# RWKV scan: gram and state products over 64 of the 128 rows, four head pairs to a step, and the scan's first load tied behind a v tile

## The chip, the cores and the metric

The kernel runs on one core of a Trainium2 chip. The metric is the device time of one execution in microseconds (us), lower is better. Three timed runs of the kernel before gave 3011.88, 3013.64 and 3014.78 us, median 3013.64.

## The reference

The model is a two-layer decoder trunk: layer 0 mixes tokens with an RG-LRU block, layer 1 with RWKV-7 time mixing; each layer then has cross-attention into 256 memory tokens and a squared-ReLU MLP (1024 tokens, width 1024, everything float32). The change is inside the RWKV-7 mixer of layer 1, in this recurrence with 16 heads of size 64:

```python
def step(state, inp):
    r_t, w_t, k_t, v_t, a_t, b_t = inp
    sa = jnp.einsum('bhij,bhj->bhi', state, a_t)
    state = (state * w_t[:, :, None, :] + sa[..., None] * b_t[:, :, None, :]
             + v_t[..., None] * k_t[:, :, None, :])
    y_t = jnp.einsum('bhij,bhj->bhi', state, r_t)
    return state, y_t
```

## The kernel before

The mixer first computes k, r and v as 128-feature tiles (`fphase`, one tile of 128 features, that is two heads, per turn), with a lot of preparation between; results go to DRAM tensors (`STd`: the two row operands of a head, b-like and k-like; `MVd`: the a-like and r-like operands; `XTd`: the inverted triangular matrices; `Vd`, `G1d`, `G2d`). In the v turns `evac_v` transposes the finished v tile, stores it to `Vd` (line 1402) and stores the gate terms to `G1d` and `G2d` (line 1416). All these transfers are issued on SyncE's queue (SP), in order.

Then the **scan** runs over 16 chunks of 64 tokens. Features of a head pair q (0 to 7) lie on the 128 partitions, head h = 0 on rows 0 to 63 and h = 1 on rows 64 to 127 (`hr[h]`). `load(n)` fetches the operands of chunks 2n and 2n+1: `st` (lines 1446, 256-byte pieces), `mv` (line 1450) and the triangular matrices (line 1452); `load_late(n)` fetches v (line 1468) and the gates (line 1472). In one chunk:

- **gram** (`scan_gram`, one chunk ahead): for each pair q and head h a product of the pair's `st` columns with `mv` of that head (line 1497). `mv` is padded: a tile `[8, 2, 2, 128]` whose other head's rows are set to zero once (line 1438), so that a product over all 128 rows gives the sums of one head. VectorE multiplies the result by masks into a tile `gt` (lines 1500 and 1503), ScalarE copies `mv` rows into it (line 1502), and the scaled `st` is transposed (line 1511) and copied in by ScalarE (line 1512).
- **W** (line 1589), one product per head over 128 rows: `gt` times `sv`, where `sv` holds the state on the head's own rows and v on the other 64. Its copy (line 1591) feeds **U** (line 1609, 64 rows by 64 columns).
- The **state product of y** (line 1594): `mv` times `sv`, over all 128 rows with the zero padding.
- VectorE writes U times a diagonal into `sv` (line 1611); **S** (line 1617) gives the new state, which VectorE adds into the next chunk's `sv` (line 1619); the output product (line 1625) adds into y.

All float32 products are two instructions each in the trace. The order of instructions on each engine is set by a scheduler that simulates the program and takes what is ready by program order; `self.behind()` pins what is issued in its block behind the last instruction of the same engine in program order. `load(0)` is called after the v turn of tile 6 (`LD = 6`); the scheduler may issue it earlier, as soon as buffers are free. Data tiles are 45 buffers `u` of 4 KB per partition, and two larger buffers `z` (of `half_big`) that hold `mv`, and before that the g2 operands of the v turns (`lowr`).

Of the kernel before, what the change touches and what calls it, by code (L numbers as in the profile page):

```python
# [10 lines left out]
ALU = mybir.AluOpType  # L11
# [1091 lines left out]
def rwkv(self, X, xt, lw_wa, lw_g, post):  # L1103
    nc, I = self.nc, self.I
    mm = nc.tensor.matmul
# [5 lines left out]
    MVd, STd = (self.dram([128, 8, 2, 1024]) for _ in range(2))  # L1111
# [13 lines left out]
    for hf in range(2):  # L1125
        o = hf * 512
# [12 lines left out]
        if hf:  # L1139
            h = maps[0][2]  # L1140
# [4 lines left out]
    h = maps[1][2]  # L1145
# [10 lines left out]
    hr = [slice(0, 64), slice(64, 128)]  # L1156
# [166 lines left out]
    def aside(step):  # L1323

        for fn, steps in ((solve_load, SL), (solve, SO), (solve_store, ST), (merge, ME), (merge_load, ML), (merge_store, MS)):
            for i, at in enumerate(steps):
                if at == step:
                    with (self.behind() if fn != solve else ExitStack()):
                        fn(i)
# [18 lines left out]
    def early(f):  # L1348
        ld[f] = self.unit()
        nc.sync.dma_start(ld[f], Pd[f * 128:f * 128 + 128, :])  # L1350
# [77 lines left out]
    cst, prs, z, mvb = {}, {}, [], []  # L1428

    def load(n):  # L1430

        if n >= 8:
            return
        ts = slice(n * 128, n * 128 + 128)
        if n < 2:
            mv = self.half_big([8, 2, 2, 128])
            for h in range(2):
                nc.gpsimd.memset(mv[hr[1 - h], :, h, :, :], 0.0)
            mvb.append(mv)
        mv = mvb[n % 2]  # L1440
        sts = []
        for g in range(2):
            st = self.unit().rearrange("p (e q w t) -> p e q w t", e=2, q=4, w=2)
            for e in range(2):
                es = slice(n * 128 + e * 64, n * 128 + e * 64 + 64)
                nc.sync.dma_start(st[:, e], STd[:, 4 * g:4 * g + 4, :, es])
            sts.append(st)
        for h in range(2):
            for w in range(2):
                nc.sync.dma_start(mv[hr[h], :, h, w, :], MVd[hr[h], :, w, ts])  # L1450
        xu = self.unit().rearrange("p (q t) -> p q t", t=128)
        nc.sync.dma_start(xu, XTd[:, :, ts])
        pcs = self.unit().rearrange("p (e q t) -> p e q t", e=2, q=8)
        for e in range(2):
            c, cs = 2 * n + e, slice(e * 64, e * 64 + 64)
            cst[c] = dict(st=[t[:, e] for t in sts], mv=mv[:, :, :, :, cs], xt=xu[:, :, cs],
                          pcs=pcs[:, e], pcc=self.pc[:, c * 8:c * 8 + 8].unsqueeze(2), gts=[])

    def load_late(n):

# [23 lines left out]
            qs = slice(4 * g, 4 * g + 4)  # L1484
            nc.gpsimd.tensor_tensor(scv[:, qs], s["st"][g], s["pcc"][:, qs].unsqueeze(3).broadcast_to([128, 4, 2, 64]), ALU.mult)

    def scan_gram(c, groups):
        if c >= 16:
            return
        s = cst[c]  # L1490
        for g in groups:
            gt = self.unit()[:, 0:768].rearrange("p (q h w) -> p q h w", q=2, h=2)
            pv = self.bank().rearrange("p (q h w) -> p q h w", q=2, h=2)
            for pp in range(2):
                q = 2 * g + pp
                for h in range(2):
                    mm(pv[:, pp, h, :], s["st"][q // 4][:, q % 4].rearrange("p w t -> p (w t)"), s["mv"][:, q, h], start=True, stop=True)
            for h in range(2):
                o = hr[1 - h]
                nc.vector.tensor_tensor(gt[o, :, h, 0:64], pv[o, :, h, 0:64],  # L1500
                                        self.mask2[o].unsqueeze(1).broadcast_to([64, 2, 64]), ALU.mult)
                nc.scalar.copy(gt[hr[h], :, h, 0:64], s["mv"][hr[h], 2 * g:2 * g + 2, h, 0, :])
            nc.vector.tensor_tensor(gt[:, :, :, 64:128], pv[:, :, :, 64:128],
                                    self.mask1[:, 0:64].unsqueeze(1).unsqueeze(1).broadcast_to([128, 2, 2, 64]), ALU.mult)
            if c < 15:
                if g % 2 == 0:
                    s["tp"] = self.bank().rearrange("p (q h i) -> p q h i", q=4, h=2)
                tp = s["tp"][:, 2 * (g % 2):2 * (g % 2) + 2]
                for pp in range(2):
                    q = 2 * g + pp  # L1510
                    nc.tensor.transpose(tp[:, pp].rearrange("p h i -> p (h i)"), s["sc"][:, q * 128:q * 128 + 128], self.ident)
                nc.scalar.copy(gt[:, :, :, 128:192], tp)
            s["gts"].append(gt)


    yq = lambda t: t.rearrange("p (q i) -> p q i", i=64)
# [18 lines left out]
    def post_norm(c):  # L1535
        s = cst[c]
        y = s["y"]
        mean, var = s["n"]
        POST(nc).tensor_tensor(yq(y[:, 0:512]), yq(y[:, 0:512]), over(var), ALU.mult)
# [17 lines left out]
    for i, fs in enumerate(turns):  # L1557
        for f in turns[i + 1] if i < 6 else []:
            early(f)
        self.fphase(I["b_w_rkv"][0, 2], fs, xv, evac_v, spread=i == 0)  # L1560
        aside(len(TURNS) + 6 + i)
        if fs[-1] == LD:
            load(0)
    scan_scale(0)
    scan_gram(0, range(4))
    load_late(0)
    self.depth, self.ahead = 2, 3
    self.psum_layout(0, 8)
# [2 lines left out]
    for c in range(16):  # L1571
        if c % 2 == 0:
            with (ExitStack() if c else self.behind()):
                load(c // 2 + 1)
                load_late(c // 2 + 1)
        s = cst[c]
        sv, gts, mv, pcc, xtc, pcs = s["sv"], s["gts"], s["mv"], s["pcc"], s["xt"], s["pcs"]
        dbv = self.db[:, 0:128].rearrange("p (q a t) -> p q a t", a=2, t=8)[:, :, c % 2, c // 2:c // 2 + 1]
        gt_of = lambda q: gts[q // 2][:, q % 2]
        W, U, S, wsb = [], [], [], []  # L1580
        y = self.unit()
        yp = self.bank()
        Y = yp.rearrange("p (q i) -> p q i", i=64)
        for m in range(2):
            ph = self.bank()
            reg = [ph[:, x * 256:x * 256 + 256].rearrange("p (q i) -> p q i", i=64) for x in range(2)]
            W.append(reg[0]); U.append(reg[1]); S.append(reg[0])
            for q, h in heads:
                mm(W[m][hr[h], q, :], gt_of(m * 4 + q)[:, h, 0:64], sv[:, m * 4 + q, h, :], start=True, stop=True)
            w_ = y[:, 512 + m * 256:768 + m * 256].rearrange("p (q i) -> p q i", i=64)  # L1590
            nc.scalar.copy(w_, W[m])
            wsb.append(w_)
            for q, h in heads:
                mm(Y[hr[h], m * 4 + q, :], mv[:, m * 4 + q, h, 1, :], sv[:, m * 4 + q, h, :],
                   start=(m == 0 and q == 0), stop=False)
            if c < 15:
                for h in range(2):
                    nc.gpsimd.tensor_tensor(pcs[hr[h], m * 4:m * 4 + 4, :], sv[hr[h], m * 4:m * 4 + 4, h, :],
                                            pcc[hr[h], m * 4:m * 4 + 4].broadcast_to([64, 4, 64]), ALU.mult)
        scan_scale(c + 1)  # L1600
        scan_gram(c + 1, (0, 1))
        if c > 1:
            flip_out(c - 2)
        if c:
            post_var(c - 1)
        for m in range(2):
            qs = slice(m * 4, m * 4 + 4)
            for q, h in heads:
                mm(U[m][hr[h], q, :], xtc[hr[h], m * 4 + q, :], wsb[m][hr[h], q, :], start=True, stop=True)
            for h in range(2):  # L1610
                nc.vector.tensor_tensor(sv[hr[h], qs, h, :], U[m][hr[h]], dbv[hr[h], qs].broadcast_to([64, 4, 64]), ALU.mult)
        scan_gram(c + 1, (2,))
        if c < 15:
            for m in range(2):
                qs = slice(m * 4, m * 4 + 4)
                for q, h in heads:
                    mm(S[m][hr[h], q, :], gt_of(m * 4 + q)[:, h, 128:192], sv[:, m * 4 + q, h, :], start=True, stop=True)
                for h in range(2):
                    nc.vector.tensor_add(cst[c + 1]["sv"][hr[h], qs, h, :], pcs[hr[h], qs, :], S[m][hr[h]])
        scan_gram(c + 1, (3,))  # L1620
        if c:
            post_norm(c - 1)
        for m in range(2):
            for q, h in heads:
                mm(Y[hr[h], m * 4 + q, :], gt_of(m * 4 + q)[:, h, 64:128], sv[:, m * 4 + q, h, :], start=False,
                   stop=(m == 1 and q == 3))
        nc.scalar.copy(y[:, 0:512], yp)
        s["y"] = y
        post_mean(c)
# [5 lines left out]
    w = I["b_w_o"][0]  # L1635
# [54 lines left out]
```

## Time and profile before

| what | value |
|---|---|
| median of three runs | 3013.64 us |
| the profiled execution | 3011.39 us, span 3009.7 us, mean granted clock 0.98 |
| busy share of the span | PE 95%, PEld 79%, DVE 60%, ACT 45%, POOL 38% |
| the scan | first W at 1817.05 us, end near 2013 us |
| distance from chunk to chunk in the middle of the scan | 12.1 and 12.3 us in turn |

PE is the matrix unit, PEld its weight loads, DVE VectorE, ACT ScalarE, POOL GpSimd, SPq SyncE's queue of transfers. A row of the timeline gives the start (us from the span's start), the length, the engine, the line and a count of merged instructions; in brackets the idle time of the engine before it and who ended it. A row of the table by stretches gives the busy time of each engine, PEclk (the granted clock of the matrix unit as a share of full speed), the busy share of the 16 DMA engines, and what they moved in GB/s.

### The profile page before, as it was taken

To read this page: it belongs to the slowest core of one execution; us is meant where nothing else is said; L and a number is where in the kernel's file an instruction comes from. 1 tells how busy PE (TensorE), PEld (TensorE's weight loads), DVE (VectorE), ACT (ScalarE), POOL (GpSimd) and SP (SyncE) were. 2 spreads that over 40 slices of the span, in tenths; PEclk is the share of its full clock that TensorE was granted. 3 is DMA by queue.
4 is the path that set the end of the run, shared out by engine and by line. 5 is a ranking of instruction groups with operands and counts; after the bars stand their busy time and mean duration, and the time that the engine had idled before them with its cause. 6 is when DMAs were issued, how large, how long until landed. Compare 5 with 4: busy or idle time off the path is not lost. (4 is left out here: it accounts for less than half of the span.)

```text
span 3009.7 us, 42878 instructions
## 1 busy us (share of the span) xinstructions
PE 2867.0 (95%) x16987; PEld 2382.3 (79%) x16987; DVE 1811.5 (60%) x1996; ACT 1357.9 (45%) x1943; POOL 1152.8 (38%) x1055
## 2 busy tenths in 40 slices
PE   7999999898999999989999899989999899999998
PEld 6888798786888878877877578878888688887886
DVE  5576552547345688867785536884354744568776
ACT  6464342535455543347442534442243545454332
POOL 2000100015666664431486225651001556667442
PEclk9999999998999999999999999999999999999999
DMA  8213261122444564332656889852312244455443
GB/s 258 73 46 94 88 210 60 57 84 70 153 154 152 213 225 146 119 116 89 183 155 183 220 246 228 175 127 96 100 50 77 84 140 154 154 210 203 158 136 119
DMA packets 382889, 421.93 MB, mean 140 GB/s; under 512 B 91248, under 2 KB 293216, under 8 KB 382688
## 3 DMA queue, kind: packets, MB, share of 16 engines
q1 hardware_dynamic: 370656, 379.19, 42.0%
q0 software_dynamic: 11568, 39.41, 3.5%
q8 instruction: 134, 2.20, 0.3%
q14 instruction: 67, 0.55, 0.1%
q10 hardware_dynamic: 464, 0.59, 0.1%
HBM read 284.31 MB, written 134.74 MB: 139 GB/s over the span
## 5 line engine op out<-in xcount | busy, mean ns | idle before, releaser
L204 DVE TENSOR_TENSOR u<-u,u 128x1024 fp32r<-128x1024 f32 (+1 forms) x518 | 818.6, 1608 | 355.3 <-ACT u L203 335.3
L304 PE MATMUL p<-u,u 128*128 128x512 f32 (+1 forms) x1920 | 716.7, 376 | 18.2 <-ACT u L203 9.5
L203 ACT CAST u<-u 128x1024 fp32r<-128x1024 f32 (+1 forms) x550 | 542.7, 1024 | 421.4 <-PE q L305 158.7
L305 PE MATMUL p<-u,u 128*128 128x512 f32 (+1 forms) x1920 | 718.1, 374 | 9.4 <-DVE u L204 9.4
L306 PE MATMUL p<-u,u 128*128 128x512 f32 (+1 forms) x1920 | 714.9, 373 | 3.8 <-DVE u L204 3.7
L304 PE MATMUL q<-u,u 128*128 128x512 f32 (+1 forms) x1632 | 642.5, 395 | 25.2 <-ACT u L203 8.3
L305 PE MATMUL q<-u,u 128*128 128x512 f32 (+1 forms) x1632 | 638.5, 392 | 7.0 <-DVE u L204 7.0
L306 PE MATMUL q<-u,u 128*128 128x512 f32 (+1 forms) x1632 | 633.6, 391 | 0.0
L304 PEld LDWEIGHTS p<-u,u 128*128 128x128 f32 x1920 | 366.5, 191 | 84.5 <-ACT u L203 13.5
L305 PEld LDWEIGHTS p<-u,u 128*128 128x128 f32 x1920 | 367.6, 191 | 74.5 <-DVE u L204 14.6
L306 PEld LDWEIGHTS p<-u,u 128*128 128x128 f32 x1920 | 367.2, 191 | 67.4 <-DVE u L204 5.8
L315 POOL TENSOR_SCALAR s<-s 128x1 f32<-128x1 f32 x98 | 36.1, 369 | 992.2 <-ACT u L313 991.2
L304 PEld LDWEIGHTS q<-u,u 128*128 128x128 f32 (+1 forms) x1632 | 308.3, 190 | 97.0 <-ACT u L203 13.5
L305 PEld LDWEIGHTS q<-u,u 128*128 128x128 f32 (+1 forms) x1632 | 308.8, 189 | 73.0 <-DVE u L204 9.3
L306 PEld LDWEIGHTS q<-u,u 128*128 128x128 f32 (+1 forms) x1632 | 308.3, 189 | 64.4
L431 POOL TENSOR_TENSOR u<-u,u 128x1024 f32<-128x1024 f32 x64 | 179.2, 2823 | 86.5 <-DVE u L204 80.4
L976 DVE TENSOR_TENSOR z<-z,q 128x512 f32<-128x512 f32 x192 | 128.9, 681 | 90.4 <-PE q L306 90.2
L204 POOL TENSOR_TENSOR u<-u,u 128x1024 fp32r<-128x1024 f32 x32 | 95.0, 2968 | 164.0 <-ACT u L203 101.9
L411 POOL TENSOR_TENSOR u<-u,u 128x512 f32<-128x512 f32 x96 | 150.8, 1580 | 2.9
L927 POOL TENSOR_TENSOR u<-u,u 128x512 f32<-128x512 f32 x32 | 47.1, 1471 | 166.2 <-ACT u L916 160.1
L304 PE MATMUL q<-z,u 128*128 128x512 f32 x256 | 102.1, 399 | 7.0 <-DVE u L611 7.0
L611 DVE SCALAR_TENSOR_TENSOR u<-p,s,u 128x1024 f32<-128x1024 f32 x24 | 30.8, 1284 | 122.1 <-ACT u L203 77.9
(260 smaller groups left out, 3536.5 us busy)
## 6 DMA issues: line engine op xcount, KB each, us to landing
u<-d SPq DMA_DIRECT2D x198, 512.0 KB, 4.4
d<-u SPq DMA_DIRECT2D x109, 512.0 KB, 3.5
d<-u POOLq DMA_DIRECT2D x68, 512.0 KB, 4.1
d<-u SPq DMA_DIRECT2D x132, 256.0 KB, 3.7
u<-in_m_w_up SPq DMA_DIRECT2D x64, 512.0 KB, 5.8
u<-in_m_w_down SPq DMA_DIRECT2D x64, 512.0 KB, 5.9
u<-in_c_w_kv SPq DMA_DIRECT2D x32, 512.0 KB, 6.5
u<-d SPq DMA_DIRECT2D x56, 256.0 KB, 6.1
```

The costliest lines, as they stand in the source:

```text
L203: self.nc.scalar.copy(hv, src)
L204: (eng or self.nc.vector).tensor_tensor(lv, src, hv, ALU.subtract)
L304: mm(o, ah, bh, start=first, stop=False, **kw)
L305: mm(o, ah, bl, start=False, stop=False, **kw)
L306: mm(o, al, bh, start=False, stop=last, **kw)
L315: nc.gpsimd.tensor_scalar(v, ss, 1.0 / n, eps, ALU.mult, ALU.add)
L411: sub = lambda o, x, y: nc.gpsimd.tensor_tensor(o, x, y, ALU.subtract)
L431: self.nc.gpsimd.tensor_tensor(f[o][i], f[x][i], f[y][i], ALU.subtract)
L611: nc.vector.scalar_tensor_tensor(o, src, r, gb, ALU.mult, ALU.mult)
L927: tt(s1, r21, r22, ALU.add)
L976: nc.vector.tensor_add(to_, to_, o)
```

## The change

The `mv` tile is unpadded: head h keeps its own 64 rows, a chunk pair's `mv` is half as large, two lie in one `z` buffer, and the zero fills on POOL go. The gram products and the state products of y read only the 64 rows of their head, so they are 64x128 and 64x64 instead of 128x128 and 128x64 (rows by weight columns). The results of h = 0 and h = 1 of the gram go to separate PSUM banks. `scan_gram` handles four pairs at once instead of two: one call does 8 products, four mask multiplies of 256 elements per row (two of them were 128), two copies of `mv`, four transposes and one copy of 512. The fourth `gt` tile goes (three tiles per chunk, sorted by purpose). `load(0)` is put behind the last instructions of the v turn of tile 6, and `mv` is fetched with two transfers over 128 rows instead of four over 64.

```diff
 def load(n):
-        if n < 2:
-            mv = self.half_big([8, 2, 2, 128])
-            for h in range(2):
-                nc.gpsimd.memset(mv[hr[1 - h], :, h, :, :], 0.0)
-            mvb.append(mv)
-        mv = mvb[n % 2]
+        if n in (0, 2):
+            t = self.half_big([2, 8, 2, 128])
+            mvb.extend(t[:, i] for i in range(2))
+        mv = mvb[n % 4]
...
-        for h in range(2):
-            for w in range(2):
-                nc.sync.dma_start(mv[hr[h], :, h, w, :], MVd[hr[h], :, w, ts])
+        for w in range(2):
+            nc.sync.dma_start(mv[:, :, w, :], MVd[:, :, w, ts])
 def scan_gram(c, g):
-                    mm(pv[:, pp, h, :], s["st"][q // 4][:, q % 4].rearrange("p w t -> p (w t)"), s["mv"][:, q, h], start=True, stop=True)
+        pv = [self.bank().rearrange("p (q w) -> p q w", q=4) for _ in range(2)]
+        for q in range(4):
             for h in range(2):
+                mm(pv[h][:, q, :], s["st"][g][hr[h], q].rearrange("p w t -> p (w t)"), mv[hr[h], 4 * g + q], start=True, stop=True)
+        for h in range(2):
+            o = hr[1 - h]
+            nc.vector.tensor_tensor(s["gt"][0][o, qs, h, :], pv[h][o, :, 0:64],
+                                    self.mask2[o].unsqueeze(1).broadcast_to([64, 4, 64]), ALU.mult)
+            nc.scalar.copy(s["gt"][0][hr[h], qs, h, :], mv[hr[h], qs, 0, :])
+        for h in range(2):
+            nc.vector.tensor_tensor(s["gt"][1][:, qs, h, :], pv[h][:, :, 64:128],
+                                    self.mask1[:, 0:64].unsqueeze(1).broadcast_to([128, 4, 64]), ALU.mult)
+        if c < 15:
+            tp = self.bank().rearrange("p (q h i) -> p q h i", q=4, h=2)
+            for q in range(4):
+                nc.tensor.transpose(tp[:, q].rearrange("p h i -> p (h i)"), s["sc"][:, (4 * g + q) * 128:(4 * g + q) * 128 + 128], self.ident)
+            nc.scalar.copy(s["gt"][2][:, qs], tp)
         if fs[-1] == LD:
-            load(0)
+            with self.behind():
+                load(0)
     scan_scale(0)
-    scan_gram(0, range(4))
+    for g in range(2):
+        scan_gram(0, g)
 # in the chunk loop
-                mm(Y[hr[h], m * 4 + q, :], mv[:, m * 4 + q, h, 1, :], sv[:, m * 4 + q, h, :],
+                mm(Y[hr[h], m * 4 + q, :], mv[hr[h], m * 4 + q, 1, :], sv[hr[h], m * 4 + q, h, :],
...
-        scan_gram(c + 1, (0, 1))
+        scan_gram(c + 1, 0)
...
-        scan_gram(c + 1, (2,))
+        scan_gram(c + 1, 1)
...
-        scan_gram(c + 1, (3,))
```

W, S and the output product read `gt[0]`, `gt[2]` and `gt[1]` instead of slices of one tile; their shapes stay.

More of the change, by code (lines that the diff above doesn't have):

```diff
@@ L1455, in load @@
             c, cs = 2 * n + e, slice(e * 64, e * 64 + 64)
-            cst[c] = dict(st=[t[:, e] for t in sts], mv=mv[:, :, :, :, cs], xt=xu[:, :, cs],
-                          pcs=pcs[:, e], pcc=self.pc[:, c * 8:c * 8 + 8].unsqueeze(2), gts=[])
+            cst[c] = dict(st=[t[:, e] for t in sts], mv=mv[:, :, :, cs], xt=xu[:, :, cs],
+                          pcs=pcs[:, e], pcc=self.pc[:, c * 8:c * 8 + 8].unsqueeze(2))
     def load_late(n):
@@ L1485, in scan_scale, with scan_gram @@
             nc.gpsimd.tensor_tensor(scv[:, qs], s["st"][g], s["pcc"][:, qs].unsqueeze(3).broadcast_to([128, 4, 2, 64]), ALU.mult)
-    def scan_gram(c, groups):
+    def scan_gram(c, g):
         if c >= 16:
@@ L1490, in scan_gram @@
         s = cst[c]
[L1491 to L1497, printed above, removed]
-            for h in range(2):
[L1499 to L1513, printed above, removed]
@@ new lines, in scan_gram @@
+        if not g:
+            s["gt"] = [self.unit().rearrange("p (q h w) -> p q h w", q=8, h=2) for _ in range(3 if c < 15 else 2)]
+        qs = slice(4 * g, 4 * g + 4)
+        mv = s["mv"]
+        pv = [self.bank().rearrange("p (q w) -> p q w", q=4) for _ in range(2)]
+        for q in range(4):
+            for h in range(2):
+                mm(pv[h][:, q, :], s["st"][g][hr[h], q].rearrange("p w t -> p (w t)"), mv[hr[h], 4 * g + q], start=True, stop=True)
[4 more added lines that the diff above has]
+            nc.scalar.copy(s["gt"][0][hr[h], qs, h, :], mv[hr[h], qs, 0, :])
@@ L1576, in rwkv @@
         s = cst[c]
-        sv, gts, mv, pcc, xtc, pcs = s["sv"], s["gts"], s["mv"], s["pcc"], s["xt"], s["pcs"]
+        sv, gt, mv, pcc, xtc, pcs = s["sv"], s["gt"], s["mv"], s["pcc"], s["xt"], s["pcs"]
         dbv = self.db[:, 0:128].rearrange("p (q a t) -> p q a t", a=2, t=8)[:, :, c % 2, c // 2:c // 2 + 1]
-        gt_of = lambda q: gts[q // 2][:, q % 2]
         W, U, S, wsb = [], [], [], []
@@ L1588, in rwkv @@
             for q, h in heads:
-                mm(W[m][hr[h], q, :], gt_of(m * 4 + q)[:, h, 0:64], sv[:, m * 4 + q, h, :], start=True, stop=True)
+                mm(W[m][hr[h], q, :], gt[0][:, m * 4 + q, h, :], sv[:, m * 4 + q, h, :], start=True, stop=True)
             w_ = y[:, 512 + m * 256:768 + m * 256].rearrange("p (q i) -> p q i", i=64)
@@ L1616, in rwkv @@
                 for q, h in heads:
-                    mm(S[m][hr[h], q, :], gt_of(m * 4 + q)[:, h, 128:192], sv[:, m * 4 + q, h, :], start=True, stop=True)
+                    mm(S[m][hr[h], q, :], gt[2][:, m * 4 + q, h, :], sv[:, m * 4 + q, h, :], start=True, stop=True)
                 for h in range(2):
                     nc.vector.tensor_add(cst[c + 1]["sv"][hr[h], qs, h, :], pcs[hr[h], qs, :], S[m][hr[h]])
-        scan_gram(c + 1, (3,))
         if c:
@@ L1624, in rwkv @@
             for q, h in heads:
-                mm(Y[hr[h], m * 4 + q, :], gt_of(m * 4 + q)[:, h, 64:128], sv[:, m * 4 + q, h, :], start=False,
+                mm(Y[hr[h], m * 4 + q, :], gt[1][:, m * 4 + q, h, :], sv[:, m * 4 + q, h, :], start=False,
                    stop=(m == 1 and q == 3))
```

## Prediction

> **What bounds the kernel now.** I read the page's busy shares first, then the table by stretches for the scan, then the waits of PE, then PE's timeline in one chunk.
>
> ```profile
> PE 2867.0 (95%) x16987; PEld 2382.3 (79%) x16987; DVE 1811.5 (60%) x1996; ACT 1357.9 (45%) x1943; POOL 1152.8 (38%) x1055
> ```
> ```profile
> 1817.00:2013.00 196.00, 182.42 (x3176) 163.04 (x3176) 156.29 (x381) 88.63 (x244) 117.18 (x143) 0.98 0.85 185
> 1904.02:1928.50 24.48, 23.33 (x415) 20.86 (x413) 20.02 (x51) 11.35 (x33) 16.56 (x21) 1.00 0.79 174
> ```
> The columns are PE, PEld, DVE, ACT, POOL, granted clock, DMA share, GB/s. PE is the bound, in the scan too: 23.33 of 24.48 us in a pair of chunks. VectorE is a close second with 20.02 us. ScalarE (11.35) and POOL (16.56) have room.
>
> ```profile
> PE q L1625 <- DVE u L1611: 5.2, 9, 2.9
> PE q L1589 <- DVE u L1619: 4.5, 7, 1.5
> PE q L1589 <- DMA u<-d: 2.4, 1, 2.4
> ```
> Over the whole scan the long waits of PE are for VectorE (9.7 us) and once, at the start, for a load. So time taken off PE counts, until VectorE is in the way.
>
> ```profile
> 1822.80 0.60 PE L1594 MATMUL q<-u,z 128*64 128x64 f32 x6
> 1823.32 0.33 PE L1609 MATMUL q<-u,u 64*64 64x64 f32 x4
> ...
> 1891.90 0.33 PE L1589 MATMUL q<-u,u 128*64 128x64 f32 x2 [0.49 <-DVE u L1619]
> 1892.07 0.28 PE L1594 MATMUL q<-u,z 128*64 128x64 f32 x2
> 1892.36 0.62 PE L1589 MATMUL q<-u,u 128*64 128x64 f32 x13
> ...
> 1893.78 0.66 PE L1594 MATMUL q<-u,z 128*64 128x64 f32 x14
> 1894.37 1.16 PE L1497 MATMUL q<-z,u 128*128 128x128 f32 x8
> 1895.46 1.15 PE L1609 MATMUL q<-u,u 64*64 64x64 f32 x32
> ...
> 1907.82 1.06 PE L1497 MATMUL q<-z,u 128*128 128x128 f32 x8
> ```
> ```profile
> L1497 PE MATMUL q<-z,u x512: 271/275/583, 1809.6 to 1997.5; 128*128 128x128 f32 x171
> L1594 PE MATMUL q<-u,z x512: 221/222/368, 1817.3 to 2004.8; 128*64 128x64 f32 x171
> ```
> The length of a matmul is modelled, so the pace is read from merged rows: eight gram instructions from 1907.82 take (1.06 - 0.275) / 7 = 0.112 us from start to start. The 64-column products (W, Y, U) run in pairs, the two heads at once: (0.66 - 0.222) / 13 = 0.034 us each, and U with 64 rows goes no faster (32 in 1.15, with a last length of 0.218: 0.030). A change of the tile's shape costs extra: the last Y before U starts at 1822.80 + 0.60 - 0.222 = 1823.18, U at 1823.32, 0.14 instead of 0.034; from Y to gram it is 1894.37 - 1894.22 = 0.15, and then the eight need 0.126 instead of 0.112 each; from gram to U 0.20 instead of 0.112. I take 0.15 us for a change, with what the first products lose.
>
> **The change part by part.**
>
> *Gram over 64 rows.* It pays if two products in different row halves run at once. One place of the trace has such products, 64x128, in the decay step:
>
> ```profile
> 1402.68 0.39 PE L305 MATMUL q<-u,u 64*128 64x512 f32 x1
> 1402.91 0.39 PE L306 MATMUL q<-u,u 64*128 64x512 f32 x1
> 1402.92 0.62 PE L304 MATMUL q<-u,u 64*128 64x512 f32 x2
> 1403.25 0.51 PE L305 MATMUL q<-u,u 64*128 64x512 f32 x2
> 1403.49 0.51 PE L306 MATMUL q<-u,u 64*128 64x512 f32 x2
> ```
> ```profile
> 1402.91 0.18 PEld L304 LDWEIGHTS q<-u,u 64*128 64x128 f32 x2
> ```
> Alone, one follows the other after 1402.91 - 1402.68 = 0.23 us; when both halves have work, seven start from 1402.91 to 1403.61 (1403.49 + 0.51 - 0.39), 0.12 apart. Two weight loads lie in one row of 0.18 us, the length of one: loads overlap as well. So the gram's 512 instructions cost 512 x 0.112 = 57.3 us now and half of that, with a small loss 29.7, afterwards: 27.6 us off PE. Bounds: 0 (no overlap for products this short) and 28.7 (exact half).
>
> *State products of y over 64 rows.* Their pace is that of U, 0.030 to 0.034: no gain. But they were of W's shape and are not any more, and the scheduler mixes them. The rows from 1891.90 show W, Y, W and further turns; I estimate from these rows seven more changes of shape in an odd chunk, three in an even one (W, Y, W, Y), ten to a pair of chunks, 80 in the scan: 80 x 0.15 = +12 us. Bounds: 0 (all grouped beside work that waits anyway) to twice this. The gram also no longer has the transposes' shape, but fewer and larger groups make up for that: 0, within 4 x 0.15 x 8 = 4.8 us either way.
>
> The Trainium skill, TensorEngine Tiling (Array Packing), section Tiling Modes, states that a change of mode, unlike one of tile, drains the engine; the 0.14 and 0.15 above agree with it. By that rule alone the state products are a pure loss, and this is the rule that speaks against the change.
>
> *VectorE.*
> ```profile
> L1500 DVE TENSOR_TENSOR u<-q,mask 64x128 f32<-64x128 f32 x120 | 34.6, 289 | 16.8 <-PE q L1497 14.0 <-DMA z<-d 0.6
> L1611 DVE TENSOR_TENSOR u<-q,db 64x256 f32<-64x256 f32 x64 | 26.9, 420 | 6.3 <-issue 3.3 <-POOL u L1598 1.4
> ```
> ```profile
> L1438 POOL MEMSET z<- x4: 1799/1804/1810, 1675.6 to 1811.6; 64x2048 f32 x4
> ```
> Eight mask multiplies of 128 elements become four of 256, which is the size in the L1611 row: per chunk 8 x 0.289 - 4 x 0.420 = 0.63, in 16 chunks 10 us off VectorE. The mask1 multiplies stay. ScalarE has fewer, longer copies; at 11.35 of 24.48 us that costs nothing, and without that slack no more than a few tenths. The zero fills (4 x 1.8 us of POOL) lie beside PE's work: 0; if POOL were the bound, 7.2 us gained.
>
> *Sum in the scan.* PE is relieved of 27.6 - 12 = 15.6 us, VectorE of 10. They alternate as the one that is late, and each waits for the other once a chunk, so the scan shortens by about the middle, 12.5 us: 0.8 us a chunk. When PE's filler between U and S gets shorter, the wait for L1611 and L1619 is what is late next. Bounds: 0 and 27.6.
>
> *The first load.*
> ```profile
> 1677.37 0.39 SPq L235 DMA_DIRECT2D u<-in_b_w_rkv  x1
> 1678.51 3.34 SPq L1450 DMA_DIRECT2D z<-d  x1
> ...
> 1788.85 4.83 SPq L1446 DMA_DIRECT2D u<-d  x4
> 1801.05 2.75 SPq L1416 DMA_DIRECT2D d<-u  x4
> 1803.89 1.69 SPq L239 DMA_DIRECT2D u<-in_b_w_o  x2
> 1806.85 2.60 SPq L1402 DMA_DIRECT2D d<-u  x4
> 1810.49 2.80 SPq L1416 DMA_DIRECT2D d<-u  x4
> 1813.35 3.08 SPq L1468 DMA_DIRECT2D u<-d  x4
> ```
> ```profile
> 1692.52 1.04 ACT L203 CAST u<-u 128x1024 fp32r<-128x1024 f32 x1 [13.02 <-DMA u<-in_b_w_rkv]
> ```
> ```profile
> 1801.00:1817.00 16.00, 12.27 (x73) 9.67 (x72) 8.38 (x18) 7.96 (x19) 6.86 (x7) 0.98 0.93 273
> ```
> `load(0)` is seven transfers of 2.6 MB: `st` four of 256 KB, `mv` two of 512 KB, the matrices 512 KB. Now `mv` is issued from 1678.51 on and `st` at 1788.85. Afterwards all stand behind the gate stores of tile 6, the L1416 at 1801.05, and so ahead of the last v tile's stores (L1402, L1416) and of the v load (L1468) that W waits for. SP is in order, so these move back by the seven issues (about 7 us at the 1.2 us of a `st` issue). The DMA engines are 0.93 busy in these 16 us at 273 GB/s: 2.6 MB more take 9.6 us, less if the two w_o loads (L239) use the earlier free place. The first W moves from 1817.05 to about 1825, and PE has nothing else to do then: +8 us. Bounds: +3 (only the issues of `mv` and the matrices are in the way) to +12 (all of the 9.6 and a quarter more).
>
> What it gives back at its old place: ScalarE waits 13.02 us there for a weight load, and PE behind it. That load was issued at 1677.37, ahead of the first `mv` at 1678.51, so I take 0; bounds 0 to -5, the 1 MB of `mv` at about 200 GB/s.
>
> *All.* -12.5 + 8 = -4.5. The profiled execution took 3011.39, which gives 3006.9; the median of the runs lies 2.25 above it: **3009**. Differences under 0.2% (6 us) can't be told from no change, and this is one.
>
> **The rivals.**
> - *The scan gains in full.* The scheduler keeps W and Y in blocks, VectorE's saving releases PE's 9.7 us of waits, and the early wait shrinks: scan -20, load +6, early -2: 3013.6 - 16 = 2998. For it: both close engines are relieved. Against: VectorE is at 20 of 24.5 us.
> - *VectorE holds the chunk.* In a chunk it needs 20.0 / 2 - 0.6 = 9.4 us in an order that PE's results set; the scan gains 3, the load costs 8: 3018.6. For it: the waits for L1611 and L1619 end at VectorE. Against: they are 9.7 us of 196.
> - *Slower: changes of shape eat the gram's gain.* With 30 more changes in a pair of chunks (W and Y alternating product by product) they cost 240 x 0.15 = 36 us against 27.6: the scan +8, the load +8: 3029.6. Level with before at (27.6 - 8) / 8 / 0.15 = 16 a pair, measurably slower from 21. For it: the single turns at 1891.90 to 1892.36. Against: blocks of 13 and 14 in the same chunk.
> - *It doesn't do what it says: the halves don't overlap.* Gram stays at 57.3, shape changes +12, load +8: 3033.6. For it: no gram-sized pair is in the trace. Against: the double load at 1402.91. The Trainium skill, TensorE: Matmul & The Clock Gate, section LDWEIGHTS, gives columns / 1.2 ns whatever the rows, so an estimated 107 ns for 128 columns; were these loads in series, the gram would gain nothing.
>
> **How the numbers follow.** My sum 0.42, the full gain 0.22, VectorE 0.11, shape changes 0.16, no overlap 0.09. My sum's own range is 3002 to 3017 (scan -18 to -6, load +3 to +12, not all at one end). The range 2994 to 3026 reaches from the full gain to most of the slower cases and leaves out about 2 in 10. Faster by over 0.2% (below 3007.6): the full gain and 0.4 of my sum, 0.38. Slower (above 3019.7): shape changes, no overlap, a little of VectorE's and mine, 0.28. Within: 0.34.
>
> **What would show it.** Sixteen gram instructions in a row start within about 1.0 us (now 1.8), with both halves in one row. Gaps of 0.15 between W and Y rows, and their count. Chunks 11.4 to 11.5 us apart instead of 12.2. `mv` and `st` issued after the stores of tile 6 near 1804, the first W near 1825. ScalarE's wait of 13 us stays. Wrong it would be if the scheduler placed the first load otherwise, or if W and Y are cut finer or coarser than now.

## The result and the profile after

The changed kernel takes 3037.34 us (median of four runs, 3034.15 to 3038.66) against 3012.76 us before: a ratio of 1.0080 with a 95% interval of 1.0063 to 1.0098. That is 0.8% slower, outside the forecast range (2994 to 3026).

In the changed kernel the lines are: gram L1496, masks L1499 and L1503, transposes L1508, W L1586, state product of y L1591, U L1606, U times the diagonal L1608, S L1614, state adds L1616, output product L1621; of the normalisation of the chunk before, L1518, L1525, L1527 and L1535 on VectorE, L1519, L1528 and L1529 on POOL. SyncE loads `st` in L1444, `mv` in L1447, the matrices in L1449, v in L1465 and the gates in L1469.

The page's busy shares of the changed kernel:

```profile
PE 2864.7 (94%) x16987; PEld 2374.1 (78%) x16987; DVE 1799.7 (59%) x1932; ACT 1342.4 (44%) x1849; POOL 1143.2 (38%) x1051
```

PE's busy time fell by 2.3 us only, and the span grew by 22.7 (3032.4 against 3009.7). The table by stretches for 100 us in the middle of the scan, before and then after:

```profile
1850.00:1950.00 100.00, 95.51 (x1663) 85.56 (x1660) 81.05 (x204) 46.69 (x133) 68.04 (x84) 1.00 0.89 195
```
```profile
1850.00:1950.00 100.00, 81.85 (x1496) 71.08 (x1496) 71.79 (x159) 34.03 (x73) 58.47 (x72) 0.90 0.84 194
```

PE went from 95.5 to 81.9 busy and its granted clock from 1.00 to 0.90; no engine is near full. 1496 matrix instructions instead of 1663 in the same time: the scan runs slower although no engine does more. From the first W of its first chunk to the first W of its last chunk it takes 195.0 us (1829.56 to 2024.55) against 184.7 (1817.05 to 2001.73). So the 22.7 us are, within 0.1, 12.5 of a later start and 10.3 of a longer scan.

**The start.** SyncE's queue in the changed kernel:

```profile
1801.45 2.83 SPq L1416 DMA_DIRECT2D d<-u  x4
1804.37 4.50 SPq L1444 DMA_DIRECT2D u<-d  x4
1808.92 2.26 SPq L1447 DMA_DIRECT2D z<-d  x2
1811.42 0.86 SPq L1449 DMA_DIRECT2D u<-d  x1
1812.37 2.60 SPq L239 DMA_DIRECT2D u<-in_b_w_o  x2
1815.06 2.95 SPq L1402 DMA_DIRECT2D d<-u  x4
1818.11 3.52 SPq L1447 DMA_DIRECT2D z<-d  x2
1821.72 4.24 SPq L1416 DMA_DIRECT2D d<-u  x4
1826.00 2.75 SPq L1465 DMA_DIRECT2D u<-d  x4
1828.80 6.35 SPq L1447 DMA_DIRECT2D z<-d  x4
```

The first load stands where the forecast put it, from 1804.37, and pushes the stores of the last v tile (L1402, L1416) and the v load (L1465) back. But two more groups of `mv` are there, at 1818.11 ahead of L1416 and L1465, and at 1828.80 ahead of the gates. They are the loads of later chunk pairs: with `mv` half as large, four pairs have room at once, and the kernel leaves the loads behind pair 1 free (with every load pinned, in experiment 2, both groups are gone from these places). PE's timeline shows the price:

```profile
1816.84 3.06 PE L1496 MATMUL q<-z,u 64*128 64x128 f32 x16 [6.70 <-DMA z<-d]
...
1829.56 0.44 PE L1586 MATMUL q<-u,u 128*64 128x64 f32 x2 [4.54 <-DMA u<-d]
```

PE waits 6.70 us for `mv` and 4.54 for v, and in between it runs at half the clock (the granted clock is 0.50 from 1812.5 to 1836.3).

**The scan.** PE, VectorE and POOL in one chunk of the changed kernel:

```profile
1915.49 1.16 PE L1496 MATMUL q<-z,u 64*128 64x128 f32 x16
...
1919.41 1.75 DVE L1608 TENSOR_TENSOR u<-q,db 64x256 f32<-64x256 f32 x4
...
1920.59 1.65 POOL L1529 TENSOR_TENSOR g<-g,nhalf 128x8 f32<-128x8 f32 x1
1920.61 1.29 PE L1614 MATMUL q<-u,u 128*64 128x64 f32 x32
1921.73 1.10 PE L1621 MATMUL q<-u,u 128*64 128x64 f32 x32
1922.28 0.69 DVE L1535 TENSOR_TENSOR u<-u,g 128x512 f32<-128x512 f32 x1 [1.11 <-POOL g L1529]
1922.98 0.43 DVE L1499 TENSOR_TENSOR u<-q,mask 64x256 f32<-64x256 f32 x1
...
1924.09 0.41 DVE L1503 TENSOR_TENSOR u<-q,mask 128x256 f32<-128x256 f32 x1
1924.42 1.76 DVE L1616 TENSOR_TENSOR u<-u,q 64x256 f32<-64x256 f32 x4
...
1924.93 1.53 PE L1586 MATMUL q<-u,u 128*64 128x64 f32 x16 [2.10 <-issue]
```

S is under way from 1920.61, yet VectorE adds it into the state (L1616) only at 1924.42: ahead of it come a piece of the normalisation (L1535) that waits 1.11 us for POOL, and the four mask multiplies of the second gram step, of which the next chunk needs two (L1499) for the second half of W only, and two (L1503) for its output product. PE's last output product ends at 1922.8, and PE has nothing more: before the change a gram step of two pairs came after S in program order (that this alone does not make the wait, experiment 9 shows). It waits 2.10 us ("issue" here: the row does not name the state adds, but W starts 0.5 us after the first of them begins). This order is new. In the trace of before the normalisation (L1539 there) stands behind at least the first state adds in the chunks 1 to 13, and between 1850 and 1950 W waits 0.5 us at most. In the changed kernel it stands ahead of all state adds in the chunks 1 to 9 and 14, and behind the first of them in 10 to 13. Why the scheduler chose so, no run shows. The table by stretches around two such waits:

```profile
1909.00:1911.00 2.00, 0.19 (x8) 0.05 (x2) 1.97 (x6) 0.59 (x1) 0.00 (x0) 1.00 0.72 162
1911.50:1914.90 3.40, 3.33 (x50) 2.82 (x48) 2.40 (x5) 1.88 (x5) 2.94 (x5) 0.51 1.00 245
...
1925.10:1928.50 3.40, 3.29 (x50) 2.81 (x48) 1.71 (x4) 1.88 (x5) 3.10 (x5) 0.50 0.00 0
```

PE idles (0.19 us busy in 2.00), and then the granted clock is 0.51 for 3.4 us; the same again after the idle before 1924.93. Seven such stretches lie between 1853 and 1956. One costs twice: about 2.1 us of idle, and an estimated 1.7 us for 3.4 us at half speed. By the length of the chunks the half speed costs less: the one chunk whose W came after such an idle without a drop, from 1938.92, took 12.64 us, against 13.6 to 14.0. The Trainium skill, TensorE: Matmul & The Clock Gate, section HAM oscillation — how this bites in real kernels, gives idle gaps above about 3.4 us as what drops the clock; here six gaps of 1.8 to 2.1 us before W are followed by a drop (one of 2.13 us, at 1936.79, is not, and the first stretch, at 1853.42, follows two gaps of 1.41 and 1.30 us). The measurement decides.

The last third of the same trace shows the counterexample, where VectorE takes the pieces in another order:

```profile
1987.38 0.41 DVE L1503 TENSOR_TENSOR u<-q,mask 128x256 f32<-128x256 f32 x1
1987.71 0.86 DVE L1616 TENSOR_TENSOR u<-u,q 64x256 f32<-64x256 f32 x2
1988.16 0.33 PE L1586 MATMUL q<-u,u 128*64 128x64 f32 x2 [0.26 <-DVE u L1616]
...
1988.60 0.75 DVE L1535 TENSOR_TENSOR u<-u,g 128x512 f32<-128x512 f32 x1
```

The masks stand ahead of the state adds here too; what has moved is L1535, with its wait for POOL. With it behind the first state adds PE waits 0.26 us (1.0 to 1.1 in every other chunk), the clock stays up, and the chunks are 12.1 and 12.6 us apart instead of 13.6 and 14.0.

### The profile page after: what moved, and what is told of

Same layout as the page of the kernel before. It is cut to its first block, busy times and chain, and to the rows that moved or that the text cites. A ratio compares the mean times of both kernels' runs of the same rounds, so it can differ in the third digit from the quotient of the medians.

```text
span 3032.4 us, 42639 instructions
## 1 busy us (share of the span) xinstructions
PE 2864.7 (94%) x16987; PEld 2374.1 (78%) x16987; DVE 1799.7 (59%) x1932; ACT 1342.4 (44%) x1849; POOL 1143.2 (38%) x1051
## 5 line engine op out<-in xcount | busy, mean ns | idle before, releaser
L304 PEld LDWEIGHTS p<-u,u 128*128 128x128 f32 x1920 | 367.4, 192 | 83.6 <-ACT u L203 12.6
L305 PEld LDWEIGHTS p<-u,u 128*128 128x128 f32 x1920 | 368.2, 192 | 74.4 <-DVE u L204 14.5
L204 DVE TENSOR_TENSOR u<-p,u 128x1024 fp32r<-128x1024 f32 x32 | 38.9, 1220 | 108.6 <-ACT u L203 108.6
```

Of the source, the lines that this page charges most:

```text
L204: (eng or self.nc.vector).tensor_tensor(lv, src, hv, ALU.subtract)
L304: mm(o, ah, bh, start=first, stop=False, **kw)
L305: mm(o, ah, bl, start=False, stop=False, **kw)
```

## The experiments

Theory: the loss is (a) the tie together with later loads that run ahead, and (b) VectorE's order ahead of the state adds, which turns PE's relief into idle time and half-clock stretches. Rival: the changes of shape on PE eat it. All ratios are to the kernel before on the same chip (medians 3013.05 to 3014.56 us). Differences between two changed kernels are differences of medians, some of them from different chips. The time of the first W, the length of the scan (from the first W of the first chunk to the first W of the last) and the distances of chunks come from one profiled execution each; a difference of a few us in a scan can be chance.

**1. The tie alone, in the kernel before.**

```diff
-            load(0)
+            with self.behind():
+                load(0)
```

> The kernel before, with load(0) put behind the last instructions of the v turn of tile 6; nothing else. Theory A (the changed kernel's 24 us are two losses: its first W comes 12.5 us later, 1829.6 instead of 1817.1, because the first load and the operands of later pairs stand in SP's queue ahead of the last v tile's stores and the v load; and the scan from the first W to the last is 195.0 instead of 184.7 us): the tie alone moves the first W to about 1825, total +8 us, scan unchanged at 185. Rival (the tie is harmless, only the operands of later pairs are in the way): first W within 2 us of 1817, total unchanged.

Measured: 3024.8 us, 1.0039 (1.0026 to 1.0052), 11.7 us more. The first W starts at 1825.41, 8.4 later than in the profile of before; another 3.7 us came in the scan, where none was expected, mostly in one chunk of 16.5 us. The forecast price of the tie (+8 on the first W) was right.

**2. The change with every load pinned.**

```diff
-            with (ExitStack() if c else self.behind()):
+            with self.behind():
                 load(c // 2 + 1)
```

> The changed kernel, with each load of a later pair put behind the last instructions before it (it was only the first of them), so that mv of pairs 1 to 3 can't go ahead of the v load and the gates. Theory A: 1 MB less ahead of the v load, the first W 4 us earlier, at about 1825.5, total 4 us less than the changed kernel; the scan stays near 195. Rival (that hoisting costs nothing, the tie is all): first W stays at 1829.6 and the total too.

Measured: 3024.44 us, 1.0040 (1.0025 to 1.0054), 12.9 us below the change. First W 1824.21 (5.4 us earlier), scan 187.7 (7.3 shorter). The shorter scan was in neither expectation: the normalisation stands ahead of the state adds in the chunks 1 to 3 only, and after the start there are two half-clock stretches, from 1863.9 and 1877.5.

**3. The change without the tie.**

```diff
-            with self.behind():
-                load(0)
+            load(0)
```

> The changed kernel with the first load free, nothing pinned: the fourth corner beside the change (3037.3), the change with pinned loads (3024.4) and the change with both (3017.6). If tie and hoisting add up, the tie costs about 7 in either state, so 3030; if the early loads of pairs 1 to 3 only collide with v's store and load because the tie put them there, 3017 to 3022, as with the pins.

Measured: 3024.44 us, 1.0031 (1.0020 to 1.0042), first W 1822.37. Between the two expectations: 12.9 us below the change, as much as the pins bring. The scan stays at 194.7.

**4. Without the tie and with every load pinned.**

```diff
-            with self.behind():
-                load(0)
+            load(0)
...
-            with (ExitStack() if c else self.behind()):
+            with self.behind():
                 load(c // 2 + 1)
```

> The changed kernel, with the scan's first load as free as in the kernel before and every later load of mv, st and the matrices pinned behind the preceding instructions of its queue. Theory (the loss is a late start, 12.5 us, plus a scan that is 10.3 us longer, of which pinning the loads took back 7): the first W comes back to about 1812 to 1818 us, the scan stays near 188 us because VectorE's order is unchanged, the time is 3012 to 3016, 0 to +0.1% against before. Rival (changes of shape between products are the cost, in every chunk): the chunks stay at 12.3 us or more and the time at 3020 or above even with the first W at 1817.

Measured: 3017.55 us, 1.0011 (1.0001 to 1.0021), 19.8 us below the change; first W 1815.36. The four corners of the first W, from the profiles: 1815.4 with neither, 1822.4 with the early loads of later pairs, 1824.2 with the tie, 1829.6 with both. The start is settled: the tie 8.9, the early loads 7.0, both 14.2. The scan is not: 191.6 us here, still 6.9 longer than before, and six half-clock stretches lie in it, from 1841.8 to 1913.4. So the time is above the first expectation and below that of the rival.

**5. The order of VectorE, in the change.** For the gram of the chunks 1 to 14 the two mask1 multiplies of the second step (L1503) are pinned behind the state adds, and in every chunk the normalisation of the chunk before.

```diff
-        for h in range(2):
-            nc.vector.tensor_tensor(s["gt"][1][:, qs, h, :], ..., ALU.mult)
+        def mask1():  # the same two instructions
+            ...
+        if g and 0 < c < 15:
+            masks.append(mask1)
+        else:
+            mask1()
...
-        if c:
-            post_norm(c - 1)
+        with self.behind():
+            if masks:
+                masks.pop()()
+            if c:
+                post_norm(c - 1)
```

> The changed kernel with its tie and its early loads, and only VectorE's order pinned in the steady chunks. Theory (start and order are two losses that add up): 14 to 16 us below the change, 3021 to 3024, with the first W at 1829 to 1831 us as in the change. Rival (the early transfers slow the chunks too, so that the order has little to give): 3028 or more.

Measured: 3015.57 us, 1.0005 (0.9996 to 1.0014), 21.8 us below the change, more than expected: the first W is at 1826.81, and the scan takes 176.8 us instead of 195.0. The tie and the early loads are all still in. Three half-clock stretches are left in the scan, after the start. One hand-over in this kernel, with the state adds L1622, W L1592, mask1 L1504 and the normalisation L1541:

```profile
1910.68 1.77 DVE L1622 TENSOR_TENSOR u<-u,q 64x256 f32<-64x256 f32 x4 [0.34 <-PE q L1620]
1911.86 0.64 PE L1592 MATMUL q<-u,u 128*64 128x64 f32 x16
1912.48 0.76 DVE L1504 TENSOR_TENSOR u<-q,mask 128x256 f32<-128x256 f32 x2
1913.15 0.68 DVE L1541 TENSOR_TENSOR u<-u,g 128x512 f32<-128x512 f32 x1
```

VectorE now waits for S (L1620) instead of the other way round, and W follows without idle time.

**6. The order, without the tie and with every load pinned** (4 and 5 together).

> As the kernel with the first load free and later loads pinned, and in the steady chunks the second gram step's mask1 multiplies and the normalisation of the chunk before are pinned on VectorE behind the state adds. Theory (VectorE does work that can wait ahead of the state adds, PE idles 2.1 us before each W): the idle before W falls below 0.7 us, the half-clock windows of the scan go, the chunks come to 11.3 to 11.8 us and the time to 2998 to 3008. Rival 1 (VectorE's sum is the bound, the order only moves its wait): chunks stay at 12.2 to 12.4 us, 3011 to 3016. Rival 2 (changes of shape on PE set the chunk): no difference from the kernel with the order of the change, within 3 us.

Measured: 3002.8 us, 0.9961 (0.9946 to 0.9976). 14.8 us below the same kernel with the change's order; scan 174.8 (instead of 191.6), chunks 11.65 us on average. Three half-clock stretches are left, from 1815.1, 1835.6 and 1890.2, where none were expected. So the two losses are each there without the other; they do not simply add up (21.8 with the early loads, 14.8 without). PE's waits between 1850 and 1950, in this kernel:

```profile
PE q L1514 <- POOL u L1482: 5.1, 6, 1.7
PE q L1619 <- DVE u L1613: 3.5, 6, 0.8
PE q L1496 <- DVE u L1504: 1.8, 4, 0.5
PE q L1591 <- issue: 1.0, 2, 0.5
```

W (L1591 here) waits 1.0 us in all, instead of 12.6 in the kernel of 4 and 12.3 in the change. What is late now is VectorE again: in every second chunk it stands for POOL.

```profile
1925.41 0.20 POOL L1525 TENSOR_SCALAR g<-g 128x8 f32<-128x8 f32 x1
1925.64 0.69 DVE L1531 TENSOR_TENSOR u<-u,g 128x512 f32<-128x512 f32 x1 [2.98 <-POOL g L1525]
```

A POOL operation of 0.20 us is late because it stands behind six others on POOL.

**7. That operation on VectorE.**

```diff
-        nc.gpsimd.tensor_scalar(mean, mean, -1.0 / 64, 0.0, ALU.mult, ALU.add)
+        nc.vector.tensor_scalar(mean, mean, -1.0 / 64, 0.0, ALU.mult, ALU.add)
```

In the kernel of 6:

> The kernel with the first load free, later loads and VectorE's order pinned (3002.8 us), and the factor -1/64 of the mean (an operation of 0.20 us on POOL) moved to VectorE. Theory (what is late now is the normalisation on VectorE, 3.0 us in every second chunk, because that small operation stands on POOL behind five of 0.8 to 1.0 us; with it the gram's masks behind it are late): the wait for POOL goes, every chunk comes to 10.6 to 11.3 us, the scan shortens by 5 to 15 us, the time is 2988 to 2998. Rival (POOL is the bound now, 35 of 50 us busy, and its scaled st holds PE's transposes): 3000 to 3005.

Measured: 2994.96 us, 0.9929 (0.9916 to 0.9941), the fastest of all, 7.8 us below 6 and 0.7% below the kernel before. Scan 168.8 us, no half-clock stretch in it, chunks 11.43 us on average between 1850 and 1950, a little above the expected 10.6 to 11.3. The operation (L1525) takes 0.17 us on VectorE in some chunks, but over 0.5 in twelve of the 16, when POOL works beside it:

```profile
1908.00 2.04 POOL L1482 TENSOR_TENSOR u<-u,pc 128x512 f32<-128x512 f32 x2
1908.08 0.99 DVE L1525 TENSOR_SCALAR g<-g 128x8 f32<-128x8 f32 x1
1909.10 1.49 DVE L1531 TENSOR_TENSOR u<-u,g 128x512 f32<-128x512 f32 x1
```

In all twelve it ends 0.03 us behind a POOL operation, and L1531 took 0.69 us in experiment 6. So a part of VectorE's busy time here is not work: its sum over the run rises by 19.6 us (1817.5 against 1797.9) for sixteen operations of 0.17. What holds them, the trace does not tell.

In the kernel of 4, with VectorE's order as in the change:

> As the kernel with the first load free and later loads pinned (3017.6 us), with VectorE's order as in the change, and the factor of the mean on VectorE. If the 3 us wait for POOL is by itself what makes VectorE late, the idle before W shrinks without any pin: chunks near 12, 3002 to 3010. If it is the masks and the normalisation ahead of the state adds, the time they wasted comes back in part only: 3010 to 3016.

Measured: 3003.09 us, 0.9956 (0.9941 to 0.9972). The early chunks keep their half-clock stretches (13.7 us apart), the later ones run at 10.7 and 11.6. The time is that of the first reading, the chunks show that the order still costs where it is bad. Without any pin of VectorE this is 14.5 us below experiment 4, as much as the pins bring (14.8); both together bring 22.6. So the order and the wait for POOL are two parts of one delay.

In the kernel before:

> The kernel before, with only the factor of the mean moved to VectorE: a control for the two others. PE is busy 95.5 of 100 us in the scan of the kernel before, so VectorE's waits cost next to nothing there: 3008 to 3016, no change. Rival (VectorE sets the chunk of the kernel before too): 3003 or less.

Measured: 3016.1 us, 1.0006 (0.9997 to 1.0015): no gain. VectorE waits for this operation in the kernel before too, up to 1.6 us, and that costs nothing while PE is 95.5% busy.

**8. The rival: the state product over 64 rows alone, in the kernel before.**

```diff
-                mm(Y[hr[h], m * 4 + q, :], mv[:, m * 4 + q, h, 1, :], sv[:, m * 4 + q, h, :],
+                mm(Y[hr[h], m * 4 + q, :], mv[hr[h], m * 4 + q, h, 1, :], sv[hr[h], m * 4 + q, h, :],
```

> The kernel before, with only the state product of y taken over the 64 rows of its head (mv stays padded, the gram stays over 128 rows, all loads as before). This measures the price of the changes of shape that were forecast at +12 us (80 changes of 0.15 us). Theory now (PE is not what sets the chunk, and shape changes cost little): 3010 to 3018. Rival (each change between W's and Y's shape costs 0.15 us on the path): 3022 to 3028.

Measured: 3015.63 us, 1.0003 (0.9993 to 1.0014), that is -2 to +4 us.

```profile
1850.00:1950.00 100.00, 97.20 (x1670) 86.44 (x1668) 81.61 (x205) 45.33 (x128) 67.45 (x83) 1.00 0.87 195
```

PE is 97.2 busy instead of 95.5, and the steady chunks take 12.28 us instead of 12.24. In PE's order W and Y follow directly on one another 199 times in the scan of before, where both have one shape, and 65 times here: with unequal shapes the scheduler keeps blocks. The rival falls as the cause of 10 us.

**9. The size of the steps.** Steps of four pairs with the padded operand, in the kernel before (the change's `scan_gram`, masks and copies, with all 128 rows and the loads of the kernel before):

```diff
-                    mm(pv[:, pp, h, :], s["st"][q // 4][:, q % 4].rearrange(...), s["mv"][:, q, h], ...)
+                mm(pv[h][:, q, :], s["st"][g][:, q].rearrange(...), mv[:, 4 * g + q, h], ...)
```

> The kernel before with padded operands and its products over all 128 rows, no tie, but four pairs to a step as in the changed kernel (two banks, masks of 256 elements, three gt tiles). Theory A (the coarse steps set an order on VectorE in which the second step's masks and the norm stand ahead of the state adds, so that W waits about 2 us a chunk with an idle PE): scan 190 to 200 us although no tile shape changes, total +5 to +15 over before. Rival B (the unpadded shapes cost it): scan 185 or less, total as before or 5 us faster.

Measured: 3018.07 us, 1.0013 (1.0004 to 1.0023). This and experiment 4 (3017.55) differ in the rows, the size of `mv` and the pins: with VectorE's order left as the scheduler chooses, the half rows bring nothing that can be seen in the time. But the two traces lose it in different places. The padded kernel has a scan of 193.6 us, as theory A expected, but not by its mechanism: one chunk of 20.25 us is in it, where the gram waits for `mv`, and W waits 0.25 us in the steady chunks. The wait of the gram (L1499 here), and a steady chunk (state adds L1618, W L1588, normalisation L1538):

```profile
1833.40 3.33 PE L1499 MATMUL q<-z,u 128*128 128x128 f32 x14 [7.18 <-DMA z<-d]
...
1917.50 0.86 DVE L1618 TENSOR_TENSOR u<-u,q 64x256 f32<-64x256 f32 x2
1917.96 0.33 PE L1588 MATMUL q<-u,u 128*64 128x64 f32 x2 [0.26 <-DVE u L1618]
1918.39 0.75 DVE L1538 TENSOR_TENSOR u<-u,g 128x512 f32<-128x512 f32 x1
```

So steps of four alone do not put the normalisation ahead of the state adds: here it stands behind the first of them in the chunks 2 to 13, in experiment 4 ahead in 1 to 7. Steady chunks take 12.5 us with full rows, without half-clock stretches; with half rows they take 13.7 and 14.0 where the normalisation stands ahead, with half-clock stretches, and 12.1 and 12.6 where it stands behind. Where it stands ahead, PE's relief became idle time, and half-clock stretches followed.

Steps of two pairs with the unpadded operand, in the change:

```diff
-        pv = [self.bank().rearrange("p (q w) -> p q w", q=4) for _ in range(2)]
-        for q in range(4):
+        for g in groups:
+            if g % 2 == 0:
+                s["pv"] = [self.bank().rearrange("p (q w) -> p q w", q=4) for _ in range(2)]
+            pv = [t[:, 2 * (g % 2):2 * (g % 2) + 2] for t in s["pv"]]
```

> The changed kernel (unpadded operand, 64-row products, tie) with the gram in steps of two pairs at the four places where the kernel before has them. Theory A: the wait before W is gone and the gram's saving on PE stays, scan 170 to 182 us, total 13 to 25 us under the changed kernel. Rival B (shape changes): scan stays at 190 or more.

Measured: 3041.15 us, 1.0089 (1.0074 to 1.0104). This says little: two steps shared their banks, and PE's gram waited 12.5 us in 14 places for VectorE's masks on them; tie and early loads were in too. So again, with the loads of experiment 4 and banks of their own:

```diff
+            pv = [self.bank()[:, 0:256].rearrange("p (q w) -> p q w", q=2) for _ in range(2)]
```

> The changed products (64 rows, unpadded operand), first load free and later loads pinned, but in gram steps of two head pairs as in the kernel before, each step with two banks of its own: two steps between W and S, one after U, one after S. Theory (the step after S is PE's filler while VectorE writes the states, and small steps hold VectorE less): the idle before W is below 1 us, chunks 11.6 to 12.1, the time 3002 to 3011. Rival (fine steps with more and smaller operations on VectorE hold the chunk, 16 mask multiplies instead of 8): chunks of 12.3 to 12.8, 3014 to 3024.

Measured: 3031.46 us, 1.0056 (1.0039 to 1.0073), slower than both expectations, with the clock at 1.00. PE's waits between 1850 and 1950:

```profile
PE q L1546 <- DVE u L1504: 4.2, 4, 1.1
PE q L1512 <- POOL u L1482: 4.1, 8, 1.3
PE q L1588 <- DVE u L1618: 3.3, 4, 1.1
```

L1546 transposes the normalised output; it waits for a mask of VectorE (L1504) whose result it doesn't read, so I take it that it waits for the bank: small steps with a bank for each row half use up the banks. Chunks are 13.0 and 14.1 us apart; these waits are not all of that, and the rest stays open.

**10. The rows alone, with the order mended.** The version of 7 with the padded operand over 128 rows (`padded_four` with the edits of 2, 5 and 7).

> The kernel before with steps of four pairs, the same order of VectorE, the factor of the mean on VectorE and every load pinned, but with the padded operand: gram and state products of y over all 128 rows. It differs from the version of 2995.0 us in the rows alone. Theory (once VectorE's order is mended, PE is late again and the 27.6 us of the gram count): PE needs 11.6 to 11.8 us a chunk, so chunks of 11.9 to 12.3 us, 3005 to 3013. Rival (the gain of that version is all from VectorE's order, the half rows bring nothing): chunks near 11.4 us, 2994 to 3000.

Measured: 3001.68 us, 0.9964 (0.9951 to 0.9977), against 2994.96 with half rows on 64-row products: the rows and the smaller operand bring 6.7 us by the medians, 10 by the ratios, between both expectations. The tables of the two, padded first:

```profile
1850.00:1950.00 100.00, 93.36 (x1778) 86.33 (x1776) 93.22 (x192) 40.25 (x88) 73.57 (x80) 1.00 0.92 199
```
```profile
1850.00:1950.00 100.00, 88.55 (x1770) 76.91 (x1768) 95.42 (x193) 39.80 (x86) 70.92 (x78) 1.00 0.96 229
```

VectorE is the fullest engine in both, or nearly so, with 93.2 and 95.4 of 100 (a part of it time in which it is held, see experiment 7), so PE's relief has little left to give: steady chunks of 11.53 and 11.43 us. VectorE is not alone: of PE's waits in the half-row version between 1850 and 1950, 6.1 us are for VectorE and 4.3 for POOL's scaled `st`. The profiled scans differ by 9.4 us; 6.6 of it is one chunk of 17.7 us in the padded kernel, where the gram waits for `mv`, 1.0 is the first chunk, and 1.8 the thirteen chunks after them:

```profile
1832.27 3.32 PE L1499 MATMUL q<-z,u 128*128 128x128 f32 x14 [5.99 <-DMA z<-d]
```

Steps of four, the pins and the moved operation give 3001.68 without one half-row product.

## Why the prediction was wrong, step by step

- **Gram over 64 rows, -27.6 us of PE: right.** The row at 1915.49 gives (1.16 - 0.272) / 15 = 0.0592 us from start to start, 512 x 0.0592 = 30.3 us against the forecast 29.7. In the version of experiment 7, with the clock up, PE's busy time over the whole run is 2838.3 us, 28.7 below the kernel before. The rival "the halves don't overlap" falls.
- **State products, +12: the price of a change right, its place on the path wrong.** The 80 changes were read from an order in which W and Y had one shape and mixed freely; with unequal shapes they follow directly on one another 65 times in the scan of the changed kernel, mostly three times a chunk. That this is near 80 is luck in part. In the fastest version the last W before Y starts at 1918.13 + 0.69 - 0.222 = 1918.60 and Y at 1918.74:

```profile
1918.13 0.69 PE L1591 MATMUL q<-u,u 128*64 128x64 f32 x16
1918.74 0.68 PE L1596 MATMUL q<-u,z 64*64 64x64 f32 x16
1919.35 1.16 PE L1496 MATMUL q<-z,u 64*128 64x128 f32 x16
```

  That is 0.14 us, as forecast (The Trainium skill, TensorEngine Tiling (Array Packing), section Tiling Modes, says that a change of mode drains the engine; the trace agrees). But it is PE's time, and experiment 8, with as many turns (65) and PE 97% busy, measured -2 to +4 us of the path.
- **VectorE, -10: right in size.** L1499 takes 64 x 0.418 = 26.8 us by its median, against 128 x 0.286 = 36.6 for the multiplies it replaces; the page's sum falls by 11.8.
- **"Sum in the scan", -12.5: this is the step that failed.** It took the relief of both engines and put about the middle of it on the path, as if their order stayed. In the trace it came out at +10.3. The sentence "the wait for L1611 and L1619 is what is late next" named the right wait (that for the state adds, L1619) and priced it at nothing. The order did not stay: the normalisation moved ahead of the state adds, PE idled up to 2.1 us before W, and half-clock stretches followed. The missing gram step behind S is not the cause by itself, as the padded kernel of experiment 9 lacks it too and W waits 0.25 us there. In place of -12.5, the runs show that VectorE's order is worth 14.8 to 21.8 us (experiments 4 to 6; 16.8 and 18.2 of the scan), and that with neither the order nor the wait for POOL mended the half rows bring nothing that can be seen in the time. Even with both mended they bring 7 to 10 with the smaller operand, not 12.5, and only about 1.8 of it in the profile after the first two chunks (experiment 10), as PE waits for VectorE and POOL there. The rival "VectorE holds the chunk" had the right place, but let the scan gain 3.
- **"The first load", +8: too small, by 4.5, and 0.5 beyond its upper bound.** The tie itself was right (+8.4 in the kernel before). What was left out is that half-size `mv` tiles free the loads of later pairs, which run ahead of v's stores and load: +7.0 alone (experiment 4). The diff showed the first part, `n in (0, 2)`; that only the load of pair 1 is pinned stands in the kernel. In the sum, seven issues at 1.2 us are 8.4 and not about 7; they took 8.0 (1804.37 to 1812.37), the forecast +8.
- **What it gives back at its old place, 0: right.** ScalarE's wait there is 12.45 us instead of 13.02:

```profile
1693.67 1.04 ACT L203 CAST u<-u 128x1024 fp32r<-128x1024 f32 x1 [12.45 <-DMA u<-in_b_w_rkv]
```

- Two rivals come near the measured time, "changes of shape eat the gram's gain" (3029.6) and "the halves don't overlap" (3033.6), both by luck: experiment 8 rules out the cause of the first, and the gram's 0.0592 us that of the second.

## What to carry to other kernels

Where two engines pass work back and forth in a loop, time taken off one of them counts only if the other hands its results over in time: look at what stands in the other's queue ahead of the hand-over before halving anything. Where a scheduler sets that queue, don't take its order from the trace of before: a change on one engine can come with another order on the other. If the change makes a buffer smaller, ask which transfers may now start early and whose queue they enter. Freeing the first load, pinning the later ones and the work that can wait behind the hand-over, and moving one 0.2 us operation to the engine that waits for it brought 2994.96 us, where the change alone had lost 0.8%.

## What the runs showed of the hardware that was not expected

Idle gaps of PE of 1.8 to 2.1 us, one in each chunk, were followed by 3.4 us at a granted clock of 0.5 in six of seven cases in the changed kernel, and with the gaps before W gone there were three such stretches left, or none (experiments 5 to 7). Sixteen W instructions take 1.12 us there (from 1927.44), against 0.69 at full clock (from 1940.55). Two row halves run at once in products as short as the gram's (0.059 us per instruction instead of 0.112, at full clock); at half clock the sixteen at 1816.84 needed 3.06 us instead of 1.16, more than twice; whether the operands came in time there, the trace doesn't tell. A 128x8 operation of 0.17 us on VectorE lasted up to 0.99 us beside a POOL operation, and the 128x512 operation behind it 1.48 us instead of 0.69 (experiment 7).
